# Group D's query and key norms, moved behind the projections of the next two tiles

## The chip, the core and the metric

The kernel runs on one core of one Trainium2 chip. The metric is device microseconds (us) of one execution; lower is better. A core has five engines, each with its own queue of instructions that it takes strictly in order: TensorE (PE, matmuls, with weight loads shown apart as PEld), VectorE (DVE), ScalarE (ACT), GpSimd (POOL), and SyncE (SP), which here issues the DMAs. They wait for each other by semaphores.

## The reference, cut to what matters

The program is two layers of a decoder trunk. Each layer mixes tokens in four parallel head groups and then runs a gated MLP. The change lies in the fourth head group, D (gated DeltaNet), at its beginning, where queries, keys and values are projected, convolved and, for queries and keys, normalised per head:

```python
def l2_norm(x):
    xf = x.astype(jnp.float32)
    return xf * lax.rsqrt(jnp.sum(xf * xf, axis=-1, keepdims=True) + EPS)

def gdn_mixer(q, k, v, beta_logit, a, z, conv_w, a_log, dt_bias, norm_g):
    qkv = jax.nn.silu(causal_dwconv(jnp.concatenate([q, k, v], axis=-1), conv_w))
    qd = l2_norm(heads(qkv[..., :HD * DK_D], HD, DK_D)) * DK_D ** -0.5
    kd = l2_norm(heads(qkv[..., HD * DK_D:2 * HD * DK_D], HD, DK_D))
    vd = heads(qkv[..., 2 * HD * DK_D:], HD, DV_D)
    beta = jax.nn.sigmoid(beta_logit.astype(jnp.float32))
    log_g = -jnp.exp(a_log.astype(jnp.float32)) * jax.nn.softplus(a.astype(jnp.float32) + dt_bias)
    o = chunk_gated_delta(qd, kd, vd, beta, log_g)
    ...
```

There are 1024 tokens, 4 heads of 64 channels in group D, a model width of 1024 and a convolution over 4 tokens.

## The kernel before

`mixing` begins each layer's token mixing with `proj_d` (line 809) and goes on with `group_d` and the projections of the other groups. `proj_d` makes six tiles of 128 channels x 1024 tokens: tiles 0 and 1 are queries, 2 and 3 keys, 4 and 5 values. Per tile `m` it does this:

- *Projection* (`proj_fm`, line 338): 48 matmuls of 512 columns, since each of 8 contraction blocks is computed as three products of high and low parts (`mm3`, line 209), for two halves of the tokens. Tile 0 also projects a small tile `misc`. The weights come by DMA into `wst`; ACT casts them to the high part (L197) and POOL subtracts to get the low part (L198). Two tiles' weights are held at a time. Each half lies in one of four PSUM banks `pd`, and ACT copies it to the tile `raw` (L378).
- *A step of other work* (`next(self.sums)`): two weight tiles of the MLP come in by DMA, POOL makes four sums or differences of them (L1555), and they go out again.
- *Convolution and SiLU*: DVE multiplies (L825) and adds three shifted products (L827); ACT takes tanh (L830); DVE finishes SiLU (L831). This goes into tile `c` (named `d` in the rows).
- *Norm*, tiles 0 to 3 only: ACT squares (L834); two matmuls with a block matrix of ones sum the squares over each head (tile `ones`, PSUM banks `pm`, line 215); ACT takes the logarithm (L839) and the exponential with factor -0.5 (L840), with a table load ahead of each; DVE scales (L841).

After the tiles follow the decay and the write strength from `misc`: eight small transposes (L219), some fifteen operations on 128 x 32 elements (among them L854 to L872), a small matmul with a triangular matrix (`du` in the rows; L215), and a round trip of the result through DRAM (`rows`), on which `group_d` builds its masks and a 32 x 32 inverse in 31 dependent steps on DVE. Between all this PE works on the next projections (`proj_tm`, 256 columns a matmul).

The order on each engine is not the order of the code: a scheduler lays the instructions of the whole program out at build time, by its own costs and priorities, so it can place the ones-matmuls of one tile inside the next tile's projection. What it laid out is fixed when the program runs.

Of the kernel before, what the change touches and what calls it, by code (L numbers as in the profile page):

```python
# [12 lines left out]
AF = mybir.ActivationFunctionType  # L13
ALU = mybir.AluOpType
# [9 lines left out]
EPS = 1e-6  # L24
# [104 lines left out]
class Body:  # L129
# [679 lines left out]
    def proj_d(self, l, hT, misc):  # L809
        nc = self.nc  # L810
        rb = self.rb
        ones = self.t("p1", "ones2", 1, [128, 128])
        nc.gpsimd.memset(ones, 0.0)
        for h in range(2):
            nc.gpsimd.memset(ones[64 * h:64 * h + 64, 64 * h:64 * h + 64], 1.0)
        fm = []
        for m in range(6):
            raw = self.pt()
            first = [(MISC, self.copy_half(misc))] if m == 0 else []
            self.proj_fm(l, hT, *first, (DQ0 + m, self.copy_half(raw)))  # L820
            next(self.sums)

            w = lambda j: self.pp[:, PP_DC + 4 * m + j:PP_DC + 4 * m + j + 1]
            c = self.t("p1", "d", ND)
            nc.vector.tensor_scalar(out=c, in0=raw, scalar1=w(3), scalar2=None, op0=ALU.mult)  # L825
            for j in range(3):
                nc.vector.scalar_tensor_tensor(out=c[:, 3 - j:S], in0=raw[:, 0:S - 3 + j], scalar=w(j), in1=c[:, 3 - j:S],  # L827
                                               op0=ALU.mult, op1=ALU.add)
            T = raw
            nc.scalar.activation(out=T, in_=c, func=AF.Tanh, scale=0.5)  # L830
            nc.vector.scalar_tensor_tensor(out=c, in0=T, scalar=1.0, in1=c, op0=ALU.add, op1=ALU.mult)  # L831
            if m < 4:
                sq = self.pt()
                nc.scalar.activation(out=sq, in_=c, func=AF.Square)  # L834
                for n in range(2):
                    sl = slice(n * 512, (n + 1) * 512)
                    p = self.ps([128, 512])
                    self.mm(p, ones, sq[:, sl])
                    nc.scalar.activation(out=sq[:, sl], in_=p, func=AF.Ln, bias=self.bias[EPS * 4])  # L839
                nc.scalar.activation(out=sq, in_=sq, func=AF.Exp, scale=-0.5)  # L840
                nc.vector.scalar_tensor_tensor(out=c, in0=c, scalar=0.125 if m < 2 else 1.0, in1=sq, op0=ALU.mult, op1=ALU.mult)  # L841
            fm.append(c)
        q, k, v = fm[0:2], fm[2:4], fm[4:6]

        pba = self.ps([128, 8, 32])
        for c in range(8):
            self.tr(pba[:, c, :], misc[32:64, c * 128:(c + 1) * 128])
        ba = self.t("p1", "ba", 1, [128, 8, 8])
        nc.vector.tensor_copy(out=ba, in_=pba[:, :, 0:8])
        bb = self.t("p1", "bb", 1, [128, 2, 32])  # L850
        c84 = lambda ap: ap.rearrange("p (c h) -> p c h", h=4)
        be = bb[:, 1, :]
        nc.scalar.activation(out=c84(be), in_=ba[:, :, 0:4], func=AF.Tanh, scale=0.5)
        nc.vector.tensor_scalar(out=be, in0=be, scalar1=0.5, scalar2=0.5, op0=ALU.mult, op1=ALU.add)  # L854
        tt = lambda o, a, b, op: nc.vector.tensor_tensor(out=o, in0=a, in1=b, op=op)
        sm = lambda nm: self.t("p1", nm, 1, [128, 32])
        x, e, u, d = sm("dx"), sm("de"), sm("du"), sm("dd")
        tt(c84(x), ba[:, :, 4:8], rb[:, None, RB_DT:RB_DT + 4].to_broadcast([128, 8, 4]), ALU.add)
        nc.scalar.activation(out=e, in_=x, func=AF.Abs)
        nc.scalar.activation(out=e, in_=e, func=AF.Exp, scale=-1.0)  # L860

        nc.vector.tensor_scalar(out=u, in0=e, scalar1=1.0, scalar2=None, op0=ALU.add)
        nc.vector.tensor_scalar(out=d, in0=u, scalar1=-1.0, scalar2=None, op0=ALU.add)
        tt(d, e, d, ALU.subtract)
        nc.vector.reciprocal(out=e, in_=u)
        tt(d, d, e, ALU.mult)
        nc.scalar.activation(out=u, in_=u, func=AF.Ln)
        tt(u, u, d, ALU.add)
        nc.vector.scalar_tensor_tensor(out=u, in0=x, scalar=0.0, in1=u, op0=ALU.max, op1=ALU.add)
        ea = self.t("p1", "ea", 1, [128, 4])  # L870
        nc.scalar.activation(out=ea, in_=rb[:, RB_ALOG:RB_ALOG + 4], func=AF.Exp)
        nc.vector.scalar_tensor_tensor(out=c84(u), in0=c84(u), scalar=-1.0, in1=ea[:, None, :].to_broadcast([128, 8, 4]),  # L872
                                       op0=ALU.mult, op1=ALU.mult)
        pb = self.ps([128, 32])
        self.mm(pb, self.cf[:, C_TRI:C_TRI + 128], u)
        bt = bb[:, 0, :]
        nc.scalar.copy(out=bt, in_=pb)
        pl = self.ps([128, 32])
        self.mm(pl, self.cf[:, C_LAST:C_LAST + 128], bt)
        ebl = self.t("p1", "ebl", 1, [128, 32])  # L880
        tt(ebl, pl, bt, ALU.subtract)
        nc.scalar.activation(out=ebl, in_=ebl, func=AF.Exp)

        pT = self.ps([64, 128])
        self.tr(pT, bb.rearrange("p a b -> p (a b)"))
        bT = self.t("p1", "bT", 1, [64, 128])
        nc.scalar.copy(out=bT, in_=pT)
        rows = self.dp.tile([64, 128], F32, tag=f"rows{l}", name=self.nm("rows"))
        nc.sync.dma_start(out=rows, in_=bT)
        return q, k, v, bb, ebl, rows  # L890
# [812 lines left out]
```

## Time and profile before

| | |
|---|---|
| time, median of 3 runs | 2936.21 us (2934.1 to 2942.85) |
| the profiled execution | 2936.43 us, its span 2934.6 us |
| mean granted TensorE clock | 0.974 of full speed |
| PE busy | 2736.2 us (93%) |
| PEld busy | 2224.1 us (76%) |
| DVE busy | 1838.8 us (63%) |
| ACT busy | 1328.4 us (45%) |
| POOL busy | 1187.8 us (40%) |

The profile is one execution. The span runs from the first to the last instruction, so the profiled execution's own time is the one to which sums over the trace are added. Busy shares are means over stages with different limits: PE at 93% says that PE bounds most of the kernel, and not which engine bounds the stretch of the change. `proj_d` of layer 0 lies at about 30 to 145 us, that of layer 1 at about 1500 to 1607 us.

### The profile page before, as it was taken

To read this page: it belongs to the slowest core of one execution; us is meant where nothing else is said; L and a number is where in the kernel's file an instruction comes from. 1 tells how busy PE (TensorE), PEld (TensorE's weight loads), DVE (VectorE), ACT (ScalarE), POOL (GpSimd) and SP (SyncE) were. 2 spreads that over 40 slices of the span, in tenths; PEclk is the share of its full clock that TensorE was granted. 3 is DMA by queue.
4 is the path that set the end of the run, shared out by engine and by line. 5 is a ranking of instruction groups with operands and counts; after the bars stand their busy time and mean duration, and the time that the engine had idled before them with its cause. 6 is when DMAs were issued, how large, how long until landed. Compare 5 with 4: busy or idle time off the path is not lost. (4 is left out here: it accounts for less than half of the span.)

```text
span 2934.6 us, 39974 instructions
## 1 busy us (share of the span) xinstructions
PE 2736.2 (93%) x14928; PEld 2224.1 (76%) x14928; DVE 1838.8 (63%) x2658; ACT 1328.4 (45%) x2422; POOL 1187.8 (40%) x1010
## 2 busy tenths in 40 slices
PE   7889888899989999999988998988999999999998
PEld 5688676677768888888767875866777778888887
DVE  4764433896477777665556643338965877776645
ACT  4423334645554444454445233346555544444543
POOL 4522453451675545300155225534526655443001
PEclk9989999999999999999999999999999999999999
DMA  5442553113443233376534315431234433333765
GB/s 188 138 109 66 177 196 113 55 51 111 138 129 112 100 108 108 105 271 195 186 131 149 106 60 197 180 106 58 67 107 144 140 108 101 100 101 104 259 193 194
DMA packets 162674, 386.02 MB, mean 132 GB/s; under 512 B 25488, under 2 KB 37040, under 8 KB 162480
## 3 DMA queue, kind: packets, MB, share of 16 engines
q1 hardware_dynamic: 162480, 383.47, 39.5%
q8 instruction: 117, 1.92, 0.3%
q14 instruction: 77, 0.63, 0.1%
HBM read 273.76 MB, written 109.64 MB: 131 GB/s over the span
## 5 line engine op out<-in xcount | busy, mean ns | idle before, releaser
L209 PE MATMUL pd<-h,wr 128*128 128x512 f32 x2608 | 662.6, 403 | 35.2 <-ACT wr L197 26.6
L209 PEld LDWEIGHTS pd<-h,wr 128*128 128x128 f32 x2608 | 491.1, 191 | 153.9 <-ACT wr L197 28.3
L198 POOL TENSOR_TENSOR wr<-wst,wr 128x512 fp32r<-128x512 f32 (+1 forms) x168 | 307.9, 1837 | 616.1 <-ACT wr L197 606.7
L197 ACT CAST wr<-wst 128x512 fp32r<-128x512 f32 (+1 forms) x260 | 196.6, 759 | 306.8 <-PE pd L209 202.0
L209 PE MATMUL pd<-wr,h 128*128 128x256 f32 x1920 | 249.3, 291 | 0.0
L209 PEld LDWEIGHTS pd<-wr,h 128*128 128x128 f32 x1920 | 242.0, 199 | 1.9 <-issue 0.5
L209 PE MATMUL pm<-h,wr 128*128 128x512 f32 x864 | 230.0, 392 | 1.7 <-DVE x L1399 1.6
L198 DVE TENSOR_TENSOR h<-st,h 128x1024 fp32r<-128x1024 f32 x120 | 152.3, 1272 | 120.9 <-ACT h L197 115.0
L209 PEld LDWEIGHTS pm<-h,wr 128*128 128x128 f32 x864 | 162.0, 188 | 39.3 <-DVE x L1399 2.4
L197 ACT CAST h<-st 128x1024 fp32r<-128x1024 f32 x120 | 125.6, 1049 | 145.8 <-PE pd L209 76.0
L209 PE MATMUL pd<-h 128*128 128x512 f32 x816 | 185.6, 389 | 0.0
L209 PE MATMUL pd<-wr,f 128*128 128x512 f32 x768 | 182.9, 395 | 0.0
L209 PEld LDWEIGHTS pd<-h 128*128 128x128 f32 x816 | 153.2, 188 | 31.8
L1337 DVE SCALAR_TENSOR_TENSOR g<-z,pp,g 128x512 f32<-128x512 f32 x176 | 164.2, 933 | 20.4 <-ACT g L1335 17.9
L209 PEld LDWEIGHTS pd<-wr,f 128*128 128x128 f32 x768 | 142.9, 188 | 32.0 <-ACT f L317 0.9
L209 PE MATMUL pm<-h 128*128 128x512 f32 x720 | 166.1, 391 | 0.7 <-DVE h L198 0.7
L1458 POOL TENSOR_TENSOR y<-y,gb 128x512 f32<-128x512 f32 x24 | 38.3, 1601 | 304.2 <-ACT fc L230 248.3
L198 DVE TENSOR_TENSOR wr<-wst,wr 128x512 fp32r<-128x512 f32 (+1 forms) x92 | 95.9, 1043 | 101.5 <-ACT wr L197 101.5
L209 PEld LDWEIGHTS pm<-h 128*128 128x128 f32 x720 | 135.5, 189 | 29.3 <-DVE h L198 1.1
L215 PE MATMUL pm<-g,g 128*128 128x128 f32 (+1 forms) x672 | 121.2, 329 | 30.1 <-issue 12.9
L215 PEld LDWEIGHTS pm<-g,g 128*128 128x128 f32 x672 | 99.3, 201 | 58.0 <-issue 30.3
L1555 POOL TENSOR_TENSOR d<-d,d 128x512 f32<-128x512 f32 x64 | 109.3, 1708 | 53.5 <-DMA d<-in_wgu_dram 48.3
(364 smaller groups left out, 5483.6 us busy)
## 6 DMA issues: line engine op xcount, KB each, us to landing
st<-gd SPq DMA_DIRECT2D x144, 256.0 KB, 3.0
gd<-g SPq DMA_DIRECT2D x88, 256.0 KB, 2.0
d<-in_wdn_dram SPq DMA_DIRECT2D x40, 512.0 KB, 5.4
td<-d SPq DMA_DIRECT2D x40, 512.0 KB, 2.7
st<-td SPq DMA_DIRECT2D x80, 256.0 KB, 3.6
ust<-in_wgu_dram SPq DMA_DIRECT2D x36, 512.0 KB, 3.7
wst<-in_wgu_dram SPq DMA_DIRECT2D x36, 512.0 KB, 3.6
st<-in_wdn_dram SPq DMA_DIRECT2D x68, 256.0 KB, 3.6
```

The lines of the kernel that those rows point to most:

```text
L197: self.marks["hi"] = self.nc.scalar.copy(out=hi, in_=src)
L198: (eng or self.nc.gpsimd).tensor_tensor(out=lo, in0=src, in1=hi.bitcast(F32), op=ALU.subtract)
L209: mm = lambda x, y, **k: self.nc.tensor.matmul(out, lhsT=x, rhs=y, skip_group_check=onto, **k)
L215: self.nc.tensor.matmul(out, lhsT=lhsT, rhs=rhs, start=start, stop=stop)
L1337: nc.vector.scalar_tensor_tensor(out=c, in0=x[:, j:j + 512], scalar=w(j), in1=c, op0=ALU.mult, op1=ALU.add)
L1458: (dve if last and n else pool).tensor_tensor(out=y[t][:, c], in0=y[t][:, c], in1=g_post[:, c], op=ALU.mult)
L1555: sub = lambda o, x, y: nc.gpsimd.tensor_tensor(out=o, in0=x, in1=y, op=ALU.subtract)
```

## The change

The norm of a tile becomes a function that is put on a list, and the list's first entry is called after the projection of the tile two places later: the norm of tile 0 after the projection of tile 2, and so on to the norm of tile 3 after that of tile 5. The square is still taken at once. All operations and their operands stay the same. In the changed file the lines behind the norm stand six lower (L1555 becomes L1561), those of the norm five lower (L841 becomes L846), those of the convolution three lower.

```diff
--- before.py
+++ after.py
@@ -813,12 +813,15 @@
         nc.gpsimd.memset(ones, 0.0)
         for h in range(2):
             nc.gpsimd.memset(ones[64 * h:64 * h + 64, 64 * h:64 * h + 64], 1.0)
-        fm = []
+        fm, norms = [], []
         for m in range(6):
             raw = self.pt()
             first = [(MISC, self.copy_half(misc))] if m == 0 else []
             self.proj_fm(l, hT, *first, (DQ0 + m, self.copy_half(raw)))
             next(self.sums)
+
+            if m > 1:
+                norms.pop(0)()
 
             w = lambda j: self.pp[:, PP_DC + 4 * m + j:PP_DC + 4 * m + j + 1]
             c = self.t("p1", "d", ND)
@@ -832,13 +835,16 @@
             if m < 4:
                 sq = self.pt()
                 nc.scalar.activation(out=sq, in_=c, func=AF.Square)
-                for n in range(2):
-                    sl = slice(n * 512, (n + 1) * 512)
-                    p = self.ps([128, 512])
-                    self.mm(p, ones, sq[:, sl])
-                    nc.scalar.activation(out=sq[:, sl], in_=p, func=AF.Ln, bias=self.bias[EPS * 4])
-                nc.scalar.activation(out=sq, in_=sq, func=AF.Exp, scale=-0.5)
-                nc.vector.scalar_tensor_tensor(out=c, in0=c, scalar=0.125 if m < 2 else 1.0, in1=sq, op0=ALU.mult, op1=ALU.mult)
+
+                def norm(c=c, m=m, sq=sq):
+                    for n in range(2):
+                        sl = slice(n * 512, (n + 1) * 512)
+                        p = self.ps([128, 512])
+                        self.mm(p, ones, sq[:, sl])
+                        nc.scalar.activation(out=sq[:, sl], in_=p, func=AF.Ln, bias=self.bias[EPS * 4])
+                    nc.scalar.activation(out=sq, in_=sq, func=AF.Exp, scale=-0.5)
+                    nc.vector.scalar_tensor_tensor(out=c, in0=c, scalar=0.125 if m < 2 else 1.0, in1=sq, op0=ALU.mult, op1=ALU.mult)
+                norms.append(norm)
             fm.append(c)
         q, k, v = fm[0:2], fm[2:4], fm[4:6]
 
```

The scheduler lays out the program anew from this code. PE, layer 0, around the ones-matmuls of the norm of tile 0 (`t_433` is the square, `pd_476` the second half of tile 1's projection). Before:

```order
L209 MATMUL pd_476<-h_89,wr_447 128x512
L215 MATMUL pm_435<-t_433,ones_75_301 128x512
L215 MATMUL pm_438<-t_433,ones_75_301 128x512
L209 MATMUL pd_476<-h_89,wr_446 128x512
L209 MATMUL pd_476<-h_90,wr_446 128x512
```

After (`pd_546` is the second half of tile 2's projection, `pd_606` the first of tile 3's):

```order
L209 MATMUL pd_546<-h_90,wr_516 128x512
L209 MATMUL pd_546<-h_89,wr_517 128x512
L215 MATMUL pm_582<-t_433,ones_75_301 128x512
L215 MATMUL pm_585<-t_433,ones_75_301 128x512
L209 MATMUL pd_606<-h_83,wr_602 128x512
```

The two matmuls stood six places before the end of tile 1's projection and now stand behind the whole of tile 2's. Those of tiles 1 to 3 move in the same way, behind the projections of tiles 3 to 5.

ACT, layer 0, from the square of tile 0 on. Before (`pd_450` and `pd_476` are the halves of tile 1's projection, `wr_618` the weights of tile 3):

```order
L834 ACTIVATE t_433<-d_426 128x1024
L378 COPY t_443<-pd_450 128x512
L839 ACT_TABLE_LOAD
L839 ACTIVATE t_433<-pm_435,bias_65 128x512
L839 ACTIVATE t_433<-pm_438,bias_65 128x512
L378 COPY t_443<-pd_476 128x512
L840 ACT_TABLE_LOAD
L840 ACTIVATE t_433<-t_433 128x1024
L197 CAST wr_618<-wst_616 128x1024
```

After (`pd_442` and `pd_468` are the halves of tile 1's projection, `wr_602` the weights of tile 3):

```order
L837 ACTIVATE t_433<-d_426 128x1024
L378 COPY t_435<-pd_442 128x512
L197 CAST wr_602<-wst_600 128x1024
L378 COPY t_435<-pd_468 128x512
L833 ACTIVATE t_435<-d_504 128x1024
L837 ACTIVATE t_511<-d_504 128x1024
L378 COPY t_513<-pd_520 128x512
L197 CAST wr_688<-wst_686 128x1024
L378 COPY t_513<-pd_546 128x512
L844 ACT_TABLE_LOAD
L844 ACTIVATE t_433<-pm_582,bias_65 128x512
```

The norm's logarithm and exponential stood between and behind the two copies of tile 1; now copy, weight cast and copy follow the square directly, as they do for every tile, and the norm of tile 0 comes after the second copy of tile 2. On DVE the scaling of a norm (L841) goes from the middle or the end of the convolution one tile later to the end of that two tiles later, ahead of its L831, and the scaling of tile 3 stands behind the last convolution, ahead of the five small operations of the decay that stood between that convolution's instructions. On PE seven more matmuls of the projection that follows stand ahead of the small matmul on `du`.

## Rows read from the trace of the kernel before

**Rows 1.** Waits, layer 0's stretch: who waited for whom, total, times, longest.

```profile
PE pm L215 <- ACT t L834: 12.4, 4, 4.6
```

**Rows 2.** The same, layer 1's stretch.

```profile
PE pm L215 <- ACT t L834: 10.6, 4, 3.7
```

**Rows 3.** Timeline of PE, layer 0: start, duration, instruction, [idle before].

```profile
32.63 27.94 PE L209 MATMUL pd<-h,wr 128*128 128x512 f32 x122
65.21 3.78 PE L215 MATMUL pm<-t,ones 128*128 128x512 f32 x4 [4.63 <-ACT t L834]
...
84.02 1.99 PE L215 MATMUL pm<-t,ones 128*128 128x512 f32 x4 [1.81 <-ACT t L834]
...
130.93 9.25 PE L209 MATMUL pd<-wr,h 128*128 128x256 f32 x75
143.10 0.41 PE L215 MATMUL pm<-du,cf 128*128 128x32 f32 x2 [2.92 <-DVE du L872]
```

**Rows 4.** Timeline of DVE, layer 0.

```profile
52.48 2.50 DVE L825 TENSOR_SCALAR d<-t,pp 128x1024 f32<-128x1024 f32 x1 [15.68 <-ACT t L378]
55.01 6.65 DVE L827 SCALAR_TENSOR_TENSOR d<-t,pp,d 128x1021 f32<-128x1021 f32 x3
62.84 1.22 DVE L831 SCALAR_TENSOR_TENSOR d<-t,d 128x1024 f32<-128x1024 f32 x1 [1.18 <-ACT t L830]
71.28 0.75 DVE L825 TENSOR_SCALAR d<-t,pp 128x1024 f32<-128x1024 f32 x1 [7.21 <-ACT t L378]
72.07 1.28 DVE L827 SCALAR_TENSOR_TENSOR d<-t,pp,d 128x1021 f32<-128x1021 f32 x1
...
74.80 5.66 DVE L827 SCALAR_TENSOR_TENSOR d<-t,pp,d 128x1022 f32<-128x1022 f32 x2
...
92.91 2.31 DVE L841 SCALAR_TENSOR_TENSOR d<-d,t 128x1024 f32<-128x1024 f32 x1
...
131.88 1.66 DVE L825 TENSOR_SCALAR d<-t,pp 128x1024 f32<-128x1024 f32 x1 [0.21 <-ACT t L378]
...
139.66 0.35 DVE L865 RECIPROCAL de<-du 128x32 f32<-128x32 f32 x1
```

**Rows 5.** Timeline of ACT, layer 0.

```profile
64.10 1.06 ACT L834 ACTIVATE t<-d 128x1024 f32<-128x1024 f32 x1 [1.29 <-DVE d L831]
...
83.87 1.06 ACT L378 COPY t<-pd 128x512 f32<-128x512 f32 x2
84.81 1.06 ACT L197 CAST wr<-wst 128x1024 fp32r<-128x1024 f32 x1
85.89 1.28 ACT L839 ACT_TABLE_LOAD   x1
...
89.77 1.06 ACT L840 ACTIVATE t<-t 128x1024 f32<-128x1024 f32 x1
```

**Rows 6.** Timeline of POOL, layer 0.

```profile
42.02 1.28 POOL L1555 TENSOR_TENSOR d<-d 128x512 f32<-128x512 f32 x1
...
52.04 2.39 POOL L198 TENSOR_TENSOR wr<-wst,wr 128x1024 fp32r<-128x1024 f32 x1 [3.05 <-ACT wr L197]
...
56.20 4.38 POOL L1555 TENSOR_TENSOR d<-d,d 128x512 f32<-128x512 f32 x2
```

**Rows 7.** Stretches: from:to, length, busy by engine, TensorE's clock, DMA.

```profile
65.00:68.00 3.00, 2.79 (x4) 1.24 (x5) 0.00 (x0) 2.59 (x4) 0.00 (x0) 0.50 0.96 279
68.00:72.00 4.00, 4.00 (x15) 2.92 (x14) 0.72 (x1) 2.02 (x4) 0.00 (x0) 0.82 0.16 64
145.00:150.00 5.00, 5.00 (x33) 5.00 (x33) 0.00 (x0) 2.18 (x3) 1.11 (x1) 0.71 0.28 79
```

**Rows 8.** Timeline of ACT and DVE, layer 1.

```profile
1528.09 1.06 ACT L834 ACTIVATE t<-d 128x1024 f32<-128x1024 f32 x1 [1.29 <-DVE d L831]
...
1594.38 2.94 DVE L825 TENSOR_SCALAR d<-t,pp 128x1024 f32<-128x1024 f32 x1
```

## The prediction, made before the changed kernel ran

> **What bounds the kernel now.** I read the waits of the matmul engine (PE) first, in the two stretches that the change touches: group D's projections of layer 0 (30 to 145 us) and of layer 1 (1500 to 1607 us). PE waits there four times for the squares that feed the norm's ones-matmuls, 12.4 us in layer 0 [rows 1] and 10.6 us in layer 1 [rows 2]. The reader is to see that nothing else holds the projections up, so these 23.0 us are what the change can aim at.
>
> Next I read PE's timeline. A tile's projection is 48 matmuls; 122 of them take 27.94 us, 0.229 us each [rows 3], so 11.0 us a tile, and a norm's two ones-matmuls (four records) take up to 1.99 us at the full clock: PE could turn a tile round every 13.0 us. Last I read the other engines for the chain that feeds PE. For tile 0 it is convolution on VectorE (DVE): L825 2.50 us, three L827 6.65 us; tanh on ScalarE (ACT) until L831 starts at 62.84; L831 1.22 us; square on ACT from 64.10 to 65.16 [rows 4, 5]. From the convolution's start at 52.48 that is 12.68 us. The next tile's convolution needs the evacuation copies, and ACT takes its work in order, so they stand behind the square. A copy takes 0.5 us and a weight cast 1.0 us from start to start (the two copies start at 83.87, the cast at 84.81) [rows 5]. So the chain's own period, 12.7 us and more plus some 2 us of copies and cast, is longer than PE's 13.0 us. That decides the forecast: with PE's wait gone, the chain DVE to ACT to DVE becomes the bound, and PE waits where it next needs the chain's end.
>
> **The change part by part.** No arithmetic goes or comes: the same eight norms, matmuls and table loads are issued. What moves is where they stand. Each norm now follows the projection two tiles later.
>
> *PE's four waits* per layer go: square 0 ends at 65.16, while in the new order PE wants it only after tile 2's projection, at 50.9 + 2 x 11.0 = 72.9 (tile 1's projection starts 80 matmuls after 32.63). With them goes, in the old order, the way round by PE: square, ones-matmuls, the rest of the projection, second copy, next convolution. It made the step from the square's end at 65.16 to the next convolution 6.1 us long (71.28) [rows 4, 5].
>
> *The new step* from square to next convolution is copy, cast, copy: 0.5 + 1.0 + 0.6 less the 0.1 that the first overlaps the square, 1.95 us. It is late next, and it holds for every tile, also where the old step was only 1 us (two copies with the cast behind them).
>
> *The chain by tiles, layer 0.* Tile 0 is as before, square until 65.16. Tile 1 starts at 67.1 and has no norm in its way; its cast and GpSimd's (POOL) weight subtraction stand just ahead of its convolution as for tile 0 (POOL L198 from 52.04, DVE L825 from 52.48) [rows 4, 6], so I give it tile 0's 12.68: square until 79.8. Tiles 2 and 3 hold the scaling of norms 0 and 1 (L841) between convolution and L831. ACT is done with such a norm 4.9 us after its first table load (85.89 to 90.83) [rows 5], well inside the convolution, so L841 runs in the wait for tanh (1.2 us). Slowed by POOL it takes 2.31 us [rows 4]: 13.8 us a tile. Tile 2: 81.75 to 95.55. Tile 3: 97.5 to 111.3. Tile 4 starts at 113.25 and ends with L831, 12.7 us later; the copies of tile 5 follow tanh and are done by then. So tile 5's convolution starts at 125.95, where it started at 131.88: 5.93 us earlier. **Layer 1** by the same steps: square 0 ends at 1529.15, tile 1 at 1531.1 to 1543.8, tile 2 1545.75 to 1559.55, tile 3 1561.5 to 1575.3, tile 4 from 1577.25, tile 5 at 1589.95 instead of 1594.38 [rows 8]: 4.43 us. Together 10.36 us.
>
> *Behind tile 5* stand norm 3's scaling, in the shadow of tanh, and the five small operations of the decay (0.2 to 0.35 us, 1.1 us in all; one at 139.66) [rows 4]. They ran between the convolution's instructions and now follow L831, half hidden by the logarithm's table load: 0.8 us lost a layer, 1.6 us in all. Its other end is nothing lost, or all 1.1 us.
>
> *Seven matmuls* of the next projection now stand ahead of the small matmul that waits for the decay (L215 at 143.10, 2.92 us of waiting) [rows 3]. At 75 in 9.25 us [rows 3] they are 0.87 us that PE does inside a wait. It counts twice a layer: the projection's end, which ACT's copies and the 32x32 inverse wait for, comes 0.87 us earlier, and 0.87 us of work is gone from what follows. 3.5 us in all; the other end is nothing, if the inverse is held by its transfers instead.
>
> *The wait moves.* PE will reach that small matmul at about 128 us (tile 5's first copy at 124, 24 matmuls, ten more) and the decay comes at about 138 (143.1 - 5.93 + 0.8): it waits 9 to 10 us there instead of 2.92, and some 4 us more in pieces before it, for square 3, the next weights and the copies. The clock is the price: after the 4.63 us wait PE ran at 0.50 of full speed (1.2 GHz) from 65 to 68 and 0.82 on average to 72, 2.2 us of work lost; after the 2.92 us wait it ran at 0.71 from 145 to 150, 1.45 us lost [rows 7]. The longer wait costs the difference, 0.75 us a layer, 1.5 us in all; bounds 0 and 4.4 us.
>
> *SP's queue* keeps its order up to the decay's round trip, apart from one small load. The tile buffers suffice: the norm holds a square two tiles longer, and the copy that takes its buffer stands behind that norm's scaling on DVE and ACT anyway.
>
> Sum: 10.36 - 1.6 + 3.5 - 1.5 = 10.8 us less. The profiled execution took 2936.43 us (span 2934.6 and 1.8 around it), beside a median of 2936.21. So **2925.6 us**.
>
> **The rivals.**
> 1. *All of the wait is gained.* If POOL's work lay beside other work of DVE, tile 1's convolution would be one L825 of 0.75 and three L827 of 1.28 us [rows 4], 4.6 us instead of 9.2; the chain would fall below PE's 13.0 us and PE would not wait. For it: the waits are PE's own [rows 1, 2]. Against it: POOL's weight subtraction starts just before each convolution. 2936.4 - 23.0 = 2913.4 us, and 2905 with the clock that these waits cost.
> 2. *DVE and POOL take strict turns.* POOL's L198 (2.39 us, 0.44 us ahead of the convolution) would hold L825 for 1.95 us, then each L827 (1.28 us) would follow an L1555 (1.28 us at 42.02) [rows 4, 6]: 1.95 + 0.75 + 3 x 2.56 = 10.4 us instead of 9.2, and L841 with the fourth L1555 2.5 instead of 2.31. Tiles 1 to 4 get 1.2, 1.4, 1.4 and 1.4 us longer, 10.8 us in two layers, and the gain is gone: 2936.4 us. This is what the Trainium skill states in "SBUF — State Buffer" (section "Who interferes with whom"): the two share one port pair as an exclusive lock, and the second to start is fully blocked. By that rule the sum would be no gain. The trace agrees for L198 and partly for the rest: three L827 took 6.65 us beside POOL, two L1555 4.38 [rows 4, 6], less than in turns.
> 3. *Slower: cast ahead of the convolution, at the slow end.* With L825 at 2.94 us [rows 8], L827 at 2.83 (two in 5.66), L841 and L831 at 2.31 [rows 4] a tile takes 17.1 us (16.0 without a norm), a period 19.1. Tile 5 would start at 139.4 and 1603.4, 7.5 and 9.0 us later than now: 2936.4 + 16.5 + 1.6 - 3.5 + 1.5 = 2952.5 us. It decides from 1.35 us a tile above my 13.25 us on average; by 2.5 us it would be measurably slower. For it: every tile now has cast and subtraction in front. Against: these durations came with a cast that fell in mid-convolution.
> 4. *Nothing moves on the chip*: the old order had already placed the ones-matmuls late (six matmuls before tile 1's end). If the chain kept its old period through the copies, 2936 us. Against it: the 6.1 us step.
>
> **How the numbers follow.** The forecast gets 0.50, with 2918 to 2932 as its own range; rival 1 0.12, rival 2 0.18, rival 3 0.12, rival 4 0.08. A measurement of this kernel can tell 0.3%, 8.8 us, so faster is below 2927.4 and slower above 2945. Of the forecast's 0.50 some 0.37 lie below 2927.4 and 0.13 above. Faster: 0.37 + 0.12 + 0.04 of rival 2 = 0.53. Slower: most of rival 3, 0.10. The same: 0.37. The range leaves out most of rival 3 and the low end of rival 1: 2909 to 2938.
>
> **What would show it.** Right: no ones-matmul waits over 1.5 us except the fourth; a wait of 7 to 11 us for the decay after tile 5 in both layers; tiles start about 15.5 us apart; L825 near 2.5 us in all tiles of a layer; tile 5's convolution near 126 and 1590 us. Wrong: tiles 13 us apart (rival 1), 17 us or more (rivals 2 and 3), or a shift that is there at the decay and gone by the end of group D.

## The result, and the profile after

The changed kernel takes 2953.54 us in the median of seven runs (2946.88 to 2957.7), the kernel before 2936.21 us (2930.85 to 2945.57, seven runs beside it). The ratio is 1.0054, with a 95% interval of 1.004 to 1.0068: slower, by 17 us where 10.8 us less were forecast. The profiled execution took 2957.41 us, span 2955.6 us, and the mean granted clock fell from 0.974 to 0.966.

In the projections it went as forecast. Tile starts on DVE in layer 0 and the decay's last operation (from the timeline: start, duration, engine, line, operation, out<-in, and in brackets the idle time ahead of it and what ended it), answering to [rows 4]:

```profile
66.18 2.50 DVE L828 TENSOR_SCALAR d<-t,pp 128x1024 f32<-128x1024 f32 x1 [3.03 <-ACT t L378]
...
81.11 2.50 DVE L828 TENSOR_SCALAR d<-t,pp 128x1024 f32<-128x1024 f32 x1 [3.03 <-ACT t L378]
...
96.76 2.41 DVE L828 TENSOR_SCALAR d<-t,pp 128x1024 f32<-128x1024 f32 x1 [3.09 <-issue]
...
112.32 2.39 DVE L828 TENSOR_SCALAR d<-t,pp 128x1024 f32<-128x1024 f32 x1 [3.09 <-issue]
...
124.66 2.85 DVE L828 TENSOR_SCALAR d<-t,pp 128x1024 f32<-128x1024 f32 x1
...
135.53 0.19 DVE L878 SCALAR_TENSOR_TENSOR du<-du,ea 128x32 f32<-128x32 f32 x1
```

This execution entered layer 0 some 0.9 us earlier than that of before (tile 0's convolution at 51.54 for 52.48). With that taken off, the forecast starts of tiles 1 to 5 are 66.2, 80.8, 96.6, 112.3 and 125.0: each is met within 0.4 us (tile 5's convolution is the line at 124.66). PE's waits in layer 0, and the decay's in layer 1, answering to [rows 1 to 3]:

```profile
110.38 1.98 PE L215 MATMUL pm<-t,ones 128*128 128x512 f32 x4 [0.56 <-ACT t L837]
114.28 0.68 PE L219 MATMUL pm<-cf,misc 32*128 32x32 f32 x8 [1.92 <-ACT t L844]
...
123.01 5.82 PE L209 MATMUL pd<-wr,h 128*128 128x256 f32 x34 [2.10 <-ACT t L378]
135.78 0.64 PE L215 MATMUL pm<-du,cf 128*128 128x32 f32 x2 [6.95 <-DVE du L878]
```
```profile
1604.75 0.64 PE L215 MATMUL pm<-du,cf 128*128 128x32 f32 x2 [8.51 <-DVE du L878]
```

The norms' 12.4 us are down to 0.56, with one wait of 1.92 us for a norm's logarithm (L844) behind it, and the wait for the decay has grown to 6.95 and 8.51 us. The decay's matmul stands at 135.78 instead of 143.10.

Where the time went is read from one query of stretches for each kernel (start:end, then the length and each engine's busy time; after POOL come PE's mean granted clock, the DMA share and GB/s). The six are group D's projections and inverse, its chunks, and the projections of groups A, B and C, in layer 0 and in layer 1. First before, then after:

```profile
50.00:215.00 165.00, 141.19 (x1093) 121.74 (x1092) 110.59 (x136) 59.98 (x80) 70.03 (x43) 0.91 0.43 133
215.00:300.00 85.00, 84.90 (x785) 68.25 (x785) 38.55 (x118) 29.50 (x76) 21.43 (x49) 0.99 0.20 65
300.00:440.00 140.00, 120.92 (x651) 96.61 (x650) 52.06 (x51) 47.16 (x68) 73.03 (x47) 0.93 0.54 194
1500.00:1680.00 180.00, 158.85 (x1192) 137.32 (x1191) 112.15 (x139) 64.98 (x90) 81.83 (x64) 0.93 0.44 136
1680.00:1760.00 80.00, 79.90 (x746) 63.73 (x746) 38.65 (x117) 28.17 (x71) 19.20 (x43) 1.00 0.20 64
1760.00:1900.00 140.00, 123.63 (x687) 99.16 (x677) 50.07 (x51) 47.81 (x70) 73.25 (x47) 0.93 0.54 194
```
```profile
50.00:215.00 165.00, 145.19 (x1145) 128.49 (x1143) 115.09 (x137) 61.66 (x85) 75.58 (x50) 0.92 0.43 137
215.00:300.00 85.00, 81.66 (x693) 65.02 (x691) 37.92 (x114) 26.07 (x65) 17.05 (x41) 0.92 0.16 52
300.00:440.00 140.00, 119.47 (x650) 93.61 (x649) 53.68 (x53) 45.67 (x70) 69.08 (x45) 0.93 0.55 195
1500.00:1680.00 180.00, 161.12 (x1209) 141.40 (x1207) 119.73 (x144) 66.70 (x95) 82.30 (x61) 0.93 0.44 139
1680.00:1760.00 80.00, 77.78 (x628) 62.79 (x630) 32.34 (x97) 23.75 (x59) 16.84 (x38) 0.85 0.18 59
1760.00:1900.00 140.00, 121.06 (x662) 92.88 (x652) 52.77 (x69) 48.15 (x77) 69.74 (x51) 0.91 0.52 185
```

PE's idle time is the length less its busy time; what the clock cost is at most the length times what is missing to 1.00. Worked out so, with a second profile of each kernel taken later:

| stretch | idle before, again | idle after, again | clock before, again | clock after, again |
|---|---|---|---|---|
| projections and inverse, layer 0 | 23.8, 23.8 | 19.8, 19.0 | 14.9, 11.6 | 13.2, 11.6 |
| group D's chunks, layer 0 | 0.1, 0.1 | 3.3, 3.5 | 0.9, 0 | 6.8, 6.8 |
| projections of C, A, B, layer 0 | 19.1, 17.7 | 20.5, 19.5 | 9.8, 12.6 | 9.8, 12.6 |
| projections and inverse, layer 1 | 21.2, 20.4 | 18.9, 18.7 | 12.6, 12.6 | 12.6, 9.0 |
| group D's chunks, layer 1 | 0.1, 0.1 | 2.2, 2.2 | 0, 0 | 12.0, 7.2 |
| projections of C, A, B, layer 1 | 16.4, 17.8 | 18.9, 20.7 | 9.8, 9.8 | 12.6, 9.8 |

The four to five microseconds of idle time gained in layer 0's projections and the two in layer 1's are there in both profiles. They are given back in the chunks and in the projections behind them, and the chunks lose the clock on top. (The stretches are cut at fixed times, so after they begin and end a few microseconds further on in the program; stretches from one operation to another are under "Why the prediction was wrong".)

Most of the chunks' loss has one place in each layer, chunk 2. PE, DVE and POOL there, first before, then after:

```profile
239.79 0.41 PE L995 MATMUL pm<-d,C 32*32 32x32 f32 x4
...
237.34 0.29 DVE L896 TENSOR_TENSOR qe<-d,ep 128x128 f32<-128x128 f32 x1 [0.49 <-PE pm L215]
238.24 1.17 DVE L1063 SCALAR_TENSOR_TENSOR DS<-DS,ep,pm 64x64 f32<-64x64 f32 x4 [0.60 <-PE pm L215]
239.43 0.78 DVE L896 TENSOR_TENSOR C<-pm,lm 32x64 f32<-32x64 f32 x3
...
241.49 0.68 DVE L410 SCALAR_TENSOR_TENSOR t<-gt,rbh 128x512 f32<-128x512 f32 x1
...
237.73 2.35 POOL L198 TENSOR_TENSOR wr<-wst,wr 128x1024 fp32r<-128x1024 f32 x1 [0.40 <-POOL U L986]
```
```profile
231.50 1.71 PE L215 MATMUL pm<-d,d 64*128 64x128 f32 x16
235.26 0.41 PE L1001 MATMUL pm<-d,C 32*32 32x32 f32 x4 [2.06 <-DVE C L902]
...
230.71 2.49 DVE L902 TENSOR_TENSOR qe<-d,ep 128x128 f32<-128x128 f32 x1 [0.57 <-PE pm L215]
233.12 0.68 DVE L410 SCALAR_TENSOR_TENSOR t<-gt,rbh 128x512 f32<-128x512 f32 x1
...
234.90 0.78 DVE L902 TENSOR_TENSOR C<-pm,lm 32x64 f32<-32x64 f32 x3
...
230.70 2.35 POOL L198 TENSOR_TENSOR wr<-wst,wr 128x1024 fp32r<-128x1024 f32 x1
```

After, POOL's subtraction for the next weights (CQ0's, cast earlier on ACT than before) starts together with `qe`, which takes 2.49 us for 0.29 and ends when the subtraction does. The gate's last multiply, which followed the C tiles before, now stands ahead of them. C comes late, PE waits 2.06 us (2.05 us in layer 1), and then runs at half clock although it is busy throughout. The two stretches behind it, after:

```profile
230.00:240.00 10.00, 7.94 (x57) 5.51 (x55) 6.28 (x15) 1.35 (x4) 2.93 (x3) 0.85 0.41 147
240.00:250.00 10.00, 10.00 (x61) 7.81 (x61) 1.70 (x4) 2.96 (x8) 0.76 (x3) 0.50 0.04 11
```

Before, PE had 1.00 in the same two. So far this is a reading of two traces; the experiments test it. Three theories: the **order theory** (the projections' gain is real, what stands ahead of C in chunk 2 makes the wait, and the half clock follows the wait); the **wait theory** (only the idle 2 us count, the half clock would come anyway); the **projection theory** (the long wait for the decay and its clock cost the time, chunk 2 does not matter).

### The profile page after: what moved, and what is told of

Read it like the earlier page. It is cut to its first block, busy times and chain, and to the rows that moved or that the text cites. A ratio compares the mean times of both kernels' runs of the same rounds, so it can differ in the third digit from the quotient of the medians.

```text
span 2955.6 us, 39976 instructions
## 1 busy us (share of the span) xinstructions
PE 2750.3 (93%) x14928; PEld 2240.8 (76%) x14928; DVE 1846.9 (62%) x2658; ACT 1327.1 (45%) x2422; POOL 1194.6 (40%) x1010
## 3 DMA queue, kind: packets, MB, share of 16 engines
q8 instruction: 117, 1.92, 0.3%
## 5 line engine op out<-in xcount | busy, mean ns | idle before, releaser
L209 PE MATMUL pd<-wr,h 128*128 128x256 f32 x1920 | 257.7, 297 | 5.1 <-ACT t L378 2.7
L209 PEld LDWEIGHTS pd<-wr,h 128*128 128x128 f32 x1920 | 249.1, 204 | 7.5 <-ACT t L378 3.1
L209 PE MATMUL pm<-hs,wr 128*128 128x512 f32 x528 | 129.1, 393 | 0.9 <-ACT x L1409 0.9
```

Source lines behind the costliest of these rows:

```text
L209: mm = lambda x, y, **k: self.nc.tensor.matmul(out, lhsT=x, rhs=y, skip_group_check=onto, **k)
```

## The experiments

An edge is a line that makes one instruction follow another on its engine; the scheduler places everything else anew, so an edge can move more than its two instructions. Ratios are to the kernel before on the same chip, where its median was 2936.83 to 2939.75 us; times from different chips compare best by these ratios (the changed kernel's is 1.0054).

**Chunk 2's order given back.**

```diff
+ if m == CQ0:
+     self.order(self.gd['do', 1], self.marks['hi'])   # chunk 1's output copy, then CQ0's cast
- nc.vector.scalar_tensor_tensor(out=v(o), ...)        # gate, not silu
+ i = nc.vector.scalar_tensor_tensor(out=v(o), ...)
+ if tp == 3:
+     self.order(self.gd['AT', 2], i)                  # chunk 2's last AT, then the gate's multiply
```

> The changed kernel with two edges that give back the order of before in chunk 2 of group D: the first cast of the next projection's weights (CQ0) stands behind chunk 1's output copy on ScalarE, and the gate's last multiply stands behind chunk 2's last AT on VectorE. Order theory (the gain in the projections is real; what stands ahead of chunk 2's C tiles makes TensorE wait 2.06 and 2.05 us and drops its clock to 0.50 for some 13 us behind): both waits and the half clock behind them go, 2 x (2.05 + 6.8) = 17.7 us, so 2930 to 2938 us. Wait theory (only the idle time counts, the half clock comes anyway): 2953.5 - 4.1 = 2949 us. Projection theory (the longer wait for the decay at the end of the projections and its clock costs it, chunk 2 does not matter): 2953 us.

Measured: 2937.82 us median of 12 runs, ratio 0.9999 (0.9984 to 1.0013). PE has no wait over 0.7 us in chunk 2, and the clock is 1.00 from 220 to 270 us and from 1660 to 1730 us. The order theory's range holds, the other two are out by 11 and 15 us. But it comes to the time of before, not to the forecast's 2925.6: a gain is still missing. The profile is of its fastest run, 2926.34 us, in which layer 1's projections also took 5.8 us less than after (67.1 us from tile 0's convolution to tile 5's, for 72.8), so that run's whole gain is not chunk 2's.

**Each edge by itself.**

> The changed kernel with one of fix_both's edges, the first cast of CQ0's weights behind chunk 1's output copy on ScalarE. If the collision of the subtraction of these weights with qe (2.49 us for 0.29) is what makes C late, TensorE's wait of 2.06 us in chunk 2 goes and the time is that of fix_both, 2936 to 2940 us; if the gate's multiply ahead of C (0.68 us, and its wait of 1 us or more for its tanh) does it, a wait of 1 to 2 us and the half clock stay, 2946 to 2953 us.

> The changed kernel with the other of fix_both's edges, the gate's last multiply behind chunk 2's last AT on VectorE. If the multiply ahead of C is what makes C late, the wait in chunk 2 goes and the time is that of fix_both, 2936 to 2940 us; if the collision of the weights' subtraction with qe does it, a wait of 1 to 2 us and half clock behind it stay, 2946 to 2953 us.

Measured: with the cast's edge 2942.01 us (ratio 1.0013, 1.0002 to 1.0025), with the gate's 2935.23 us (0.9985, 0.9973 to 0.9997). Either alone takes the wait away in its profile, so the expectations, which each gave the wait to one of the two alone, both missed; the times lie 2 us over and 0.8 us under the range of the case that the wait goes. DVE and POOL with the gate's edge:

```profile
229.18 0.29 DVE L905 TENSOR_TENSOR qe<-d,ep 128x128 f32<-128x128 f32 x1 [0.56 <-PE pm L216]
...
231.27 0.78 DVE L905 TENSOR_TENSOR C<-pm,lm 32x64 f32<-32x64 f32 x3
...
229.19 2.50 POOL L199 TENSOR_TENSOR wr<-wst,wr 128x1024 fp32r<-128x1024 f32 x1
```

The subtraction still starts together with `qe`, but here `qe` is 0.01 us ahead (after, it was 0.01 us behind) and takes 0.29 us; the subtraction takes 2.50 for 2.35. C starts 2.1 us behind `qe`'s start, as before, where it was 4.2 after. In the runs that keep both the collision and the multiply ahead of C, `qe` is the first in some layers too (layer 1 of the changed kernel's second profile, both layers of the two runs that fill the wait, layer 0 of the run with one layer alone). There the multiply takes 2.83 or 2.84 us for 0.68, and C is as late. With the cast's edge the multiply still stands ahead, at 0.69 us, the subtraction falls on neither, and C comes 1.7 us behind `qe`'s start. So the collision makes C late, on whichever of the two it falls; without the multiply ahead it found nothing to hold. What the gate's edge does where `qe` comes second, no profile shows. The gate's edge is even the better of the two by 7 us; why the cast's costs that much was not found.

**The wait filled with work.**

```diff
+ if m == CKV and n == 0 and k == 2:
+     self.order(i, self.c2)        # nine matmuls of CKV, then chunk 2's first product on C
```

> The changed kernel with one edge on TensorE alone: seven more matmuls of the CKV projection, whose weights are there, go ahead of chunk 2's first product on C, so that TensorE works through some 1.7 of the 2.06 us in which it waited; VectorE's and GpSimd's collision stays. Order theory: the idle time and the half clock behind it go, 2 x (1.7 + 6.8) = 17 us, so 2934 to 2940 us, with the granted clock near 1.0 from 237 to 250 us. Wait theory: the work that fills the wait is only moved, 2953.5 - 3.4 = 2950 us, clock still 0.50 there. Projection theory: 2953 us.

Measured: 2943.63 us (ratio 1.0013, 0.9999 to 1.0028), 10 us under the changed kernel, 4 over the order theory's range. The wait is only partly gone:

```profile
234.28 0.62 PE L1004 MATMUL pm<-d,C 32*32 32x32 f32 x12 [0.53 <-DVE C L905]
...
239.56 1.08 PE L1025 MATMUL pm<-V,C 64*64 64x64 f32 x8 [2.12 <-issue]
```

The matmuls that were brought forward are missing a few products later, where PE now waits 2.12 us, and the half clock stands behind that wait (0.56 from 240 to 250 us). The collision fell on the multiply here, which took 2.84 us for 0.68.

```profile
229.04 2.84 DVE L413 SCALAR_TENSOR_TENSOR t<-gt,rbh 128x512 f32<-128x512 f32 x1
```

**The wait filled with dummies.**

```diff
+ if c == 2:
+     for _ in range(27):
+         self.mm(p.rearrange("p h t -> p (h t)"), ident_h, v[0][:, cl])
```

> The changed kernel with 27 dummy matmuls of 128 columns on TensorE, about 2.9 us, in chunk 2 of group D ahead of its first product on C, in both layers; they write the same accumulator, which the products then overwrite. What stands ahead of C on VectorE, the collision and the time of C stay. Idle theory (TensorE's empty 2 us are what the half clock behind chunk 2 follows): the stretch of 13.7 us at 0.50 behind chunk 2 goes in both layers, 2953.5 - 2 x 6.8 = 2940 us, with the dummies costing 0 to 1 us more than the wait did. Pace theory (the half clock comes with the late C and the work behind it, empty or not): clock 0.50 stays from 237 to 250 us, 2953 to 2956 us.

Measured: 2950.88 us (1.0037, 1.0024 to 1.005). That is between the two theories' numbers and decides for neither. The dummies were mis-sized: 6.29 us, not 2.9. PE is full from 230 to 240 us at clock 1.00, with C as late as ever (4.2 us behind `qe`'s start), but a new wait of 2.37 us follows:

```profile
231.59 6.29 PE L215 MATMUL pm<-d,ident_h 128*128 128x128 f32 x54
237.81 0.44 PE L1004 MATMUL pm<-d,C 32*32 32x32 f32 x16
...
243.14 1.08 PE L1023 MATMUL pm<-V,C 64*64 64x64 f32 x8 [2.37 <-issue]
```
```profile
230.00:240.00 10.00, 10.00 (x115) 9.03 (x115) 5.25 (x13) 0.93 (x3) 1.66 (x1) 1.00 0.54 159
240.00:250.00 10.00, 7.63 (x34) 5.91 (x34) 1.97 (x4) 2.54 (x7) 0.76 (x3) 0.60 0.00 0
```

The half clock moved with the idle time and not with the late C, which speaks for the idle theory and does not show it.

**One layer alone.**

```diff
- if m > 1:
+ if m > 1 and l == 0:
      norms.pop(0)()
...
+ if l != 0:
+     norms.pop(0)()
```

> The norms follow two tiles later in layer 0 alone; layer 1 is as before. Order theory: -7.3 us at the decay and +9.6 us in chunk 2 of layer 0 and nothing in layer 1, so 2936.2 + 2 to 3.5 = 2938 to 2940 us, with a TensorE wait of about 2 us and a half clock behind it near 237 us and none near 1708 us. Projection theory: half of the 17.3 us, 2945 us, already there at the end of layer 0's projections.

Measured: 2945.99 us (1.0028, 1.0016 to 1.004), at the projection theory's number and 6 us over the order theory's. The profile has the order theory's marks: a wait of 2.02 us on C in chunk 2, 0.50 from 240 to 250 us, no wait over 0.4 us in layer 1's chunks, and the decay's matmul at 137.9, 5.2 us before that of before. So chunk 2's marks follow the layer that was changed, and the net cost expected for the layer, read off one trace as a difference of two shifts, was too small. What the rest of it is was not found. The projection theory's own mark, a loss that is there at the end of layer 0's projections, is absent.

**The late multiply put into the kernel before.**

```diff
+ if tp == 3:
+     self.order(i, self.gd['C', 2])   # the gate's multiply, then chunk 2's first C
```

> The kernel before with one edge that gives it the changed kernel's place of the gate's last multiply: ahead of chunk 2's first C on VectorE. Nothing of the norms is moved. Order theory: TensorE waits 1 to 3 us for C in chunk 2 of both layers and runs at half clock behind it, 2 x (2 + 6.8) = 17.6 us, so 2946 to 2956 us. Wait theory: 2936.2 + 2 to 6 us = 2938 to 2942 us. Projection theory: 2936 us.

Measured: 2950.42 us (1.0033, 1.0021 to 1.0045), inside the order theory's range, by another road. PE waits 0.74 us in chunk 2 and the clock there stays at 1.00: the subtraction had begun 1.7 us before the multiply, so only its end fell on it (1.19 us for 0.68), and that does not make C late enough. The edge also moved rows of ACT's, PE's, POOL's and SP's order behind the chunks; which of these costs its 11 us stays open.

**The weights of groups A and B.** Both the changed kernel and the mended one wait more for these weights than before: 13.21 + 2.06 + 2.85 us near 360 us before, 4.81 + 14.19 + 1.21 after. PE and POOL after:

```profile
363.71 12.16 PE L209 MATMUL pd<-h,wr 128*128 128x512 f32 x46 [4.81 <-POOL wr L198]
...
391.97 1.22 PE L209 MATMUL pd<-h,wr 128*128 128x512 f32 x2 [14.19 <-ACT wr L197]
394.40 5.82 PE L209 MATMUL pd<-h,wr 128*128 128x512 f32 x18 [1.21 <-POOL wr L198]
```
```profile
353.50 1.29 POOL L1561 TENSOR_TENSOR d<-d,d 128x512 f32<-128x512 f32 x1 [7.26 <-DMA d<-in_wgu_dram]
...
357.10 3.82 POOL L1561 TENSOR_TENSOR d<-d,d 128x512 f32<-128x512 f32 x2
360.88 2.78 POOL L198 TENSOR_TENSOR wr<-wst,wr 128x1024 fp32r<-128x1024 f32 x1
```

POOL is idle for 7.26 us, then does a step of the down sums, and only then the subtraction that PE waits for (its cast stood on ACT at 347.42). The next loads stand on SP behind the stores of these sums.

```diff
+ p = {AF1: -1, AQ1: 0, BQ: 1}[m]
+ self.order(self.marks["lo"], self.subs[11 + p])        # subtraction, then a step of the sums
+ if m != AF1:
+     self.order(self.marks["load"], self.puts[10 + p])  # load, then the stores of a step
```

> The changed kernel with chunk 2 mended as in fix_both, and the weights of the group A and B projections moved ahead in their queues: the subtraction of AF1's weights ahead of a step of the down sums on GpSimd, the loads of AQ1's and BQ's weights ahead of the stores of those sums on SyncE. Third-place theory (fix_both's gain of some 10 us at the projections is partly eaten near 351 and 1800 us, where TensorE waits 4.7 + 14.3 + 1.2 and 5.2 + 13.5 + 1.2 us for these weights against 13.2 + 2.1 + 2.9 and 13.4 + 1.9 + 0.9 before): the first wait goes and the second shrinks by 5 to 10 us, 2 x (5 + 5 to 10), so 2908 to 2920 us, and 8 to 11 us under the kernel before with the same loads. Absorption theory (the gain is given back whatever stands there, by the granted clock alone): 2915 to 2930 us, and within 3 us of the kernel before with the same loads.

> The kernel before with the same edges on the weights of the group A and B projections as fix_load, the norms and chunk 2 as before. The waits of 13.2 + 2.1 + 2.9 us near 358 us shrink by 5 to 10 us in each layer: 2919 to 2930 us by both theories. Third-place theory: fix_load is 8 to 11 us faster than this one; absorption theory: within 3 us of it.

> The changed kernel with the gate's last multiply behind chunk 2's last AT, without the edge on CQ0's cast, and with the edges of fix_load on the group A and B weights. At the same granted clock the gate's edge alone stood some 6 us under both edges, so if that holds with the loads too, 2927.1 - 6 = 2921 us; if the loads' gain and the gate's are the same time, the time is that of fix_load, 2925 to 2930 us.

Measured: with both edges of chunk 2 and these, 2927.13 us (0.9964, 0.995 to 0.9977): **faster than both kernels**. PE's waits there, in layer 0, fall from some 20 to 13 us:

```profile
367.53 1.22 PE L210 MATMUL pd<-h,wr 128*128 128x512 f32 x2 [4.95 <-ACT wr L198]
369.97 23.68 PE L210 MATMUL pd<-h,wr 128*128 128x512 f32 x94 [1.21 <-POOL wr L199]
397.45 0.73 PE L210 MATMUL pd<-h,wr 128*128 128x512 f32 x2 [3.81 <-ACT wr L198]
401.45 8.76 PE L210 MATMUL pd<-h,wr 128*128 128x512 f32 x30 [3.27 <-POOL wr L199]
```

The time is 7 us over the third-place theory's range and inside the absorption theory's; the second condition, the time against the kernel before with the same loads, neither theory met. In the kernel before the same edges made it slower, 2946.48 us (1.0033, 1.0021 to 1.0046), against an expected gain by every theory, so the difference of 19 us between the two is no clean price of the change. With the gate's edge alone and the loads, 2931.89 us (0.9989, 0.9978 to 0.9999), over both numbers that were expected: the loads add nothing to the gate's edge alone (0.9985).

**A second profile of each kernel.**

> The changed kernel itself, for a second profile. If chunk 2's wait and the half clock behind it belong to the kernel's order, they are there again in both layers (a wait of 2.0 to 2.1 us near 233 and 1706 us, clock 0.50 for 7 us or more behind each) and the time is 2947 to 2958 us. If they were an accident of the one profile, at least one of the half-clock stretches is gone.

> The kernel before itself, for a second profile. If the half clock in the projections belongs to its four waits of two to five us, some 3 to 7 us at 0.50 stand behind two or three of them in each layer again, none between 215 and 300 us, and the time is 2931 to 2946 us.

Measured: 2949.87 and 2938.16 us. The changed kernel waits 2.06 and 2.02 us in chunk 2 again, with clock 0.50 from 240 to 250 us and a like stretch in layer 1; before has neither. What did not come again is a longer half clock near 1680 us, which of the two profiles only the first shows (0.50 from 1680 to 1690 us): the order alone does not bring it. Of before's four waits for the norms in layer 0, only the first has half clock behind it the second time (0.51 from 65 to 68 us), fewer than expected.

## Why the prediction was wrong

The steps up to the decay were right in their mechanism:

- PE's waits for the norms went, except a small one for the fourth. Tile 5's convolution came at 124.66, 6.3 us earlier by this execution's own start (forecast 5.93). In layer 1 it came at 1593.59 instead of 1594.38 [rows 8], in an execution that entered that layer 4.3 us later (first square at 1532.38 for 1528.09 [rows 8]): 5.1 us (forecast 4.43). That is against the profile that the forecast was read from. From tile 0's convolution to tile 5's the profiles of before give 79.4 and 76.3 us in layer 0 and 77.0 and 76.3 in layer 1, those of after 73.1 and 72.8 both times: 6.3 and 4.2 us gained by the first pair, 3.2 and 3.4 by the second. So the size of layer 0's term hangs in part on one slower execution of before.
- The new wait for the decay was 7 to 8.5 us where 9 to 10 were given; its clock cost no more than before (13.2 and 11.6 for 14.9 and 11.6 us in layer 0), where 1.5 us were set aside. No run separates the 3.5 us of the seven matmuls or the 1.6 us of the five small operations.
- Rivals 1 and 2 are out by the same tile starts. Rival 3's 2952.5 us is the measured time by coincidence: its mechanism, tiles 19 us apart, did not happen, they are 12 to 16 apart. Rival 4 is out too.

**The step that failed is the one from the decay to the end**: the sum carried the shift of the decay's end to the kernel's end at full value and set everything behind it to no change. The prediction looked at the order up to the decay's round trip only. Its own last sentence names what happened, a shift that is there at the decay and gone by the end of group D, but none of its rivals gave that a price. The runs show in its place:

- *Chunk 2*, both layers: 2.05 us of wait and 6.8 us of clock behind it, 17.7 us in all, in both profiles of after. The time from `qe` to `qe` in the table below says the same (17.5 us). Giving back the order there takes off 15.7 us (2953.54 to 2937.82); in its profile chunk 2's part is 7.2 and 7.8 us of the two layers. That the collision makes C late is shown by the cast's edge, which takes it away and leaves the multiply ahead.
- *The weights of groups A and B*: 1.6 and 2.7 us more idle time in layers 0 and 1 than before, averaged over the two profiles of each. With loads and subtraction moved ahead as well, the kernel gains 12.0 us on before (2939.11 to 2927.13). That this is the norms' gain set free is not shown, since those edges are a change of their own, and in the kernel before they cost.
- *Idle time and clock over the whole span.* PE's busy time went from 2736.2 to 2750.3 us and its idle time (span less busy) from 198.4 to 205.3; in the second profiles from 2736.7 to 2740.7 and from 199.7 to 207.4. Idle time is 7 to 8 us of the loss in both pairs. The rest, 14 us in one and 4 in the other, is the same 14928 matmul records taking longer, as they do at the lower clock: the seven runs of after had granted clocks of 0.965 to 0.971 (mean 0.968), the 73 runs of before beside the experiments 0.970 to 0.978 (mean 0.974).

The change of time, after less before, from one operation to the same operation (the start of tile 0's convolution, and that of the second `qe` of chunks 2 and 4), shows where the forecast was lost:

| from | to | first profiles | second profiles |
|---|---|---|---|
| tile 0, layer 0 | chunk 2 | -5.7 | -5.2 |
| chunk 2 | chunk 4 | +8.9 | +8.9 |
| chunk 4 | tile 0, layer 1 | +1.1 | -0.9 |
| tile 0, layer 1 | chunk 2 | +1.7 | -4.4 |
| chunk 2 | chunk 4 | +8.7 | +8.6 |
| chunk 4 | the end | +7.3 | +4.1 |

Up to chunk 2 the second profiles gain 9.6 us of the forecast's 10.8. In the first, layer 1's gain is hidden by the longer half clock near 1680 us. Then chunk 2 takes back more than the gain in each layer.

Left open: whether idle time by itself brings the half clock. In all profiles taken here, each wait of 2.0 us or more inside group D's chunks (nine of them, in after, its second profile, one layer alone, and the two that filled the wait) has 0.50 behind it for 3 to 14 us, and in the 19 layers without such a wait no half clock begins in the chunks, but for the one behind the wait for the inverse ahead of them. Both fillings only moved the wait, so none of these runs has the same late C with no wait at all. Nor is it shown what keeps the mended kernel at the time of before, when its chunk 2 is mended and the projections' gain is there.

## What to carry to other kernels

When a scheduler places the instructions, a gain at one place is a new order at all later ones: compare the order to the end of the kernel, engine by engine, and look where something now stands ahead of an operation that the bounding engine waits for. Price a new wait on the matmul engine with the clock behind it, which here cost three times the wait itself (6.8 us behind 2.05). And a kernel whose edges move its time by 10 us either way can hide a right forecast of 10 us; the place to verify it is the stretch from one operation to another, in more than one profile, and not the total.

## What the hardware showed that was not expected

- A wait of 2.06 us, after some 28 us in which PE had no wait over 0.4 us, is followed by half clock (1.2 GHz) that lasts from 237 to 251 us while PE is busy all the time. Waits of 1.9 to 2.1 us in the projections (at 112 and 121 us after, at 116 before) mostly have much less behind them.
- POOL's subtraction with two inputs in SBUF stops a small DVE operation for its whole length: `qe` 2.49 us for 0.29, the gate's multiply 2.84 for 0.68. This is what the Trainium skill says in "SBUF — State Buffer" (section "Who interferes with whom"): the two engines' shared port pair is an exclusive lock, and the one that comes second is fully blocked. The trace agrees here. Which one waits was decided by 0.01 us (`qe` at 230.71 behind the subtraction at 230.70: 2.49 us; at 229.18 ahead of one at 229.19: 0.29). Not every DVE operation is stopped: before, the DS updates and the C tiles ran beside the subtraction (237.73 to 240.08) and took 1.17 and 0.78 us, as long as after without it (1.15 and 0.78). The convolutions and POOL's sums take turns too, but a turn of one L827 and one L1555 takes some 2.2 us (6.65 for three, 4.38 for two [rows 4, 6]) and not the 2.56 that rival 2 gave it from their lengths alone; the forecast's durations came from those rows and held.
